# Rotary embedding joined in PSUM by TensorE, and GpSimd left with gathers only, in a two-layer diffusion backbone step

## The chip, the cores and the metric

One Trainium2 chip, one of its cores. The metric is the device time of one launch in microseconds (us): three runs of the kernel before took 4050.77, 4027.24 and 4058.07 us, median 4050.77. The profile comes from one more execution, which has its own time.

## The reference, cut to what matters

One inference step of two layers over 128 context tokens ("prompt") and 512 latent tokens ("sample"), width 1024, all in float32. Each layer is a mixer (layer 0: grouped-query attention and retention; layer 1: differential and windowed attention) followed by a PEER channel mixer, in which each token has 8 heads that choose 16 of 16384 single-neuron experts. What the change touches:

```python
def ada(x, gain, shift, scale):
    return rmsnorm(x, gain) * (1.0 + scale[:, None, :]) + shift[:, None, :]

def apply_rope(x, cos, sin):           # latent tokens only
    x1, x2 = x[..., :half], x[..., half:]
    return concatenate([x1 * cos - x2 * sin, x1 * sin + x2 * cos], axis=-1)

# retention, per chunk: qc * q_dec[..., None] meets the carried state s
o = intra + einsum('bhqd,bhdv->bhqv', qc * q_dec[..., None], s)

# PEER, per block of 128 tokens
a = einsum('td,thkd->thk', xb, u[ib])       # rows of u chosen by index
w = gb * gelu(a)
out = einsum('thk,thkd->td', w, v[ib])      # rows of v chosen by index
```

## The kernel before

Activations stand transposed, 128 features by tokens, in float32. The sample's projections split each operand into a rounded high part and a residue (`hhi`, `hlo`, `whi`, `wlo`) and take three TensorE matmuls for one product (L478). The program runs one after the other: mixer 0 (0 to about 716 us of the profile), routing 0 (to 1310), dense 0 (to 2200), mixer 1 (to 2640), routing 1 (to 3230) and dense 1 (to the end). The prompt's work is woven in between, and so are the gathers.

The PEER mixer is done in two ways. For three blocks of 128 sample tokens it multiplies densely with all experts (L1434, L1457). For the prompt's block and the last sample block, in each layer, it gathers the chosen rows: 128 rows of `u` per token and then 128 rows of `v`, each step an indirect DMA that GpSimd issues (L1323) into one of 8 buffers `row`, and one VectorE instruction of 128x1024 that consumes it (L1336 for `u`, L1340 for `v`). GpSimd may issue the next gather when VectorE has given a buffer back, so GpSimd, the DMA and VectorE form a ring. In mixer 1 VectorE consumes 171 gathers; in mixer 0 the ring runs from about 344 us on.

`chunk` (L558) loads a weight, projects into a PSUM bank of tag `mm` (two banks; the even mixer's q and k use tag `S`), runs the postponed work of the chunk before (`flush`, the list `pend`), and then hands the bank to its reader. The order on each engine is fixed when the program is built: a scheduler with a timeline of its own orders the instructions, and two pins keep gathers behind the instruction last written on GpSimd and VectorE (`after`, L1299).

Three jobs share GpSimd with the gathers:

- `rope` (L501), 18 times on the sample: 4 q chunks and k in mixer 0; k of the windowed attention and 4 times `cq`, `ck`, `dq` in mixer 1. `y` is in SBUF (VectorE scales it at L627 or L692 in mixer 0, ScalarE copies it out of PSUM at L957 in mixer 1). TensorE swaps the halves (`perm`, L505), GpSimd multiplies `y` by cos (L507), VectorE multiplies the swapped one by sin out of PSUM (L509), GpSimd adds (L511), in two instructions of 64 partitions where the two heads go to two tensors (`kz0`, `kz1`, and the two halves of `ck`).
- `qd` (L803): the decayed queries of the retention, 8 times in mixer 0.
- `hlo` of every third of the eight slices in `ada` (L446 to L450, `HL = 3`), 2 in each of the four sample norms, with a second ScalarE pass over the slice (L449). The other six are one VectorE instruction (L452).

Of the kernel before, what the change touches and what calls it, by code (L numbers as in the profile page):

```python
# [53 lines left out]
TRM = 1  # L54
RE = 1
DGB = 2
HL = 3
HN = 1
MHB = 1
ML = 1  # L60
# [96 lines left out]
def _consts():  # L157
    C = {}
    p = np.arange(128)
    C["ident"] = np.eye(128, dtype=np.float32)  # L160
    half = p // 64
    swap = p ^ 32
    perm = np.zeros((128, 128), np.float32)
    perm[swap, p] = 1.0
    C["perm"] = perm
    same = (half[:, None] == half[None, :]).astype(np.float32)
    C["center"] = (np.eye(128) - same / 64.0).astype(np.float32)
    sel = np.zeros((128, 2), np.float32)
    sel[p, half] = 1.0 / 64.0
    C["sel"] = sel  # L170
    inv = (np.float32(10000.0) ** (-np.arange(16, dtype=np.float32) / np.float32(16))).astype(np.float32)
    t = np.arange(NS)
    row = (t // 64).astype(np.float32)
    col = (t % 64).astype(np.float32)
    ang = np.concatenate([row[:, None] * inv, col[:, None] * inv], axis=-1).astype(np.float32)
    cos, sin = np.cos(ang).T, np.sin(ang).T
    d = p % 64
    C["cos"] = cos[d % 32].astype(np.float32)
    C["sin"] = (sin[d % 32] * np.where(d < 32, -1.0, 1.0)[:, None]).astype(np.float32)
    delta = np.arange(896)[None, :] - p[:, None] - 384  # L180
    C["delta"] = delta.astype(np.float32)
    C["qf"] = np.tile(np.arange(1, NS + 1, dtype=np.float32)[None], (128, 1))
    C["qb"] = np.tile((NS - np.arange(NS, dtype=np.float32))[None], (128, 1))
    C["kr"] = np.stack([127.0 - p, p], axis=1).astype(np.float32)
    kq = p[None, :] - p[:, None]
    C["mprev"] = np.where(kq >= 0, 0.0, NEG).astype(np.float32)
    C["mnext"] = np.where(kq <= 0, 0.0, NEG).astype(np.float32)

    first = [[o for o, ab in enumerate(CAND) if ab[0] == a][0] for a in range(16)]
    C["first"] = np.tile(np.array(first, np.float32)[None], (128, 1))  # L190
    C["firstk"] = np.tile(np.array(first, np.float16)[None, :, None], (128, 1, 16))
    C["iotak"] = np.tile(np.arange(16, dtype=np.float16)[None, :, None], (128, 1, 16))
    C["iota2"] = np.tile(np.arange(128, dtype=np.float16)[None, :, None], (128, 1, 2))
    return {k: np.ascontiguousarray(v) for k, v in C.items()}
# [54 lines left out]
class K:  # L249
# [186 lines left out]
    def ada(self, st, gs, sh):  # L436

        nc = self.nc
        r = st.r0 if st.r0 is not None else self.rstd_x(st)
        st.r0 = None  # L440
        pb = self.rstd_bcast(st, r)
        h = self.pair_tile(st, "h")
        for k in range(8):
            t = self.wk.tile([128, st.T], F32, tag="t2", name="ada_t", bufs=6)
            nc.vector.scalar_tensor_tensor(t, st.x[:, k], gs[:, k:k + 1], pb[:, :st.T], op0=ALU.mult, op1=ALU.mult)
            if st.sample:  # L446
                nc.scalar.activation(h[0][:, k], t, AF.Identity, bias=sh[:, k:k + 1])
                if HL and k % HL == HL - 1:
                    nc.scalar.activation(t, t, AF.Identity, bias=sh[:, k:k + 1])  # L449
                    nc.gpsimd.tensor_tensor(h[1][:, k], t, h[0][:, k], op=ALU.subtract)  # L450
                    continue
                nc.vector.scalar_tensor_tensor(h[1][:, k], t, sh[:, k:k + 1], h[0][:, k],  # L452
                                               op0=ALU.add, op1=ALU.subtract)
            else:
                nc.scalar.activation(h[:, k], t, AF.Identity, bias=sh[:, k:k + 1])
        return h
# [41 lines left out]
                nc.tensor.matmul(pb[w * g:w * g + w, i * 128:(i + 1) * 128], r[:, o + g:o + g + 1].to_broadcast([128, w]),  # L498
                                 self.c["ident"], start=True, stop=True, tile_position=(0, w * g))

    def rope(self, y, outs):  # L501

        nc, c = self.nc, self.c
        ps = self.bank("mm")
        nc.tensor.matmul(ps, c["perm"], y, start=True, stop=True)  # L505
        t1 = self.wk.tile([128, NS], F32, tag="t2", name="rp1", bufs=6)
        nc.gpsimd.tensor_tensor(t1, y, c["cos"], op=ALU.mult)  # L507
        t2 = self.wk.tile([128, NS], F32, tag="t2", name="rp2", bufs=6)
        nc.vector.tensor_tensor(t2, ps, c["sin"], op=ALU.mult)  # L509
        for dst, sl in outs:  # L510
            nc.gpsimd.tensor_tensor(dst, t1[sl], t2[sl], op=ALU.add)  # L511

    def vtrans(self, src, st, dsts):

# [91 lines left out]
    def even(self, sts):  # L606
# [10 lines left out]
        for m in (4, 0, 1, 2, 3):  # L617
            for st, p in self.chunk(sts, "win0", m, CS):
                n = 2 * st.nt
                if m == 4:  # L620
                    st.kraw = self.ph.tile([128, st.T], F32, tag="rq" + st.name, name="kraw", bufs=2)
                    st.sv = self.ph.tile([128, 5 * n], F32, tag="sv" + st.name, name="sv")
                if m == 4:
                    nc.vector.tensor_copy(st.kraw, p)
                else:
                    y = self.wk.tile([128, st.T], F32, tag="t2", name="y", bufs=6) if st.sample else st.mo[:, m]
                    nc.vector.tensor_scalar(y, p, c["gqk"][:, 0:1], None, op0=ALU.mult)  # L627
                sq = self.wk.tile([128, st.T], F32, tag="t2", name="sq", bufs=6)
                nc.scalar.activation(sq, p, AF.Square)

                def rest(st=st, sq=sq, m=m, n=n):
                    pv = self.small(st)
                    self.head_sums(pv, 0, sq, st, c["sel"])
                    nc.vector.tensor_copy(st.sv[:, m * n:(m + 1) * n], pv[:, :n])
                    if m == 3:
                        st.r = self.rsq(st.sv, 5 * n)
                        st.r8 = self.ph.tile([128, 5 * n], F32, tag="r8" + st.name, name="r8")
                        nc.vector.tensor_scalar(st.r8, st.r, 0.125, None, op0=ALU.mult)

                st.pend.append(rest)  # L640
                if m < 4 and st.sample:
                    st.pend.append(lambda y=y, st=st, m=m: self.rope(y, [(st.mo[:, m], slice(0, 128))]))
# [36 lines left out]
    def qk_finish(self, st, m):  # L679
# [10 lines left out]
        if st.sample:  # L690
            y = self.wk.tile([128, T], F32, tag="t2", name="y", bufs=6)
            nc.vector.scalar_tensor_tensor(y, raw, gain, pb[:, :T], op0=ALU.mult, op1=ALU.mult)  # L692
            self.rope(y, outs)
        else:
            for dst, sl in outs:
                nc.vector.scalar_tensor_tensor(dst, raw[sl], gain[sl], pb[sl, :T], op0=ALU.mult, op1=ALU.mult)
# [89 lines left out]
    def retention(self, st, cch):  # L786
# [4 lines left out]
        if st.sample:  # L791
# [5 lines left out]
            for d, rn in ((0, "qf"), (1, "qb")):  # L797
# [2 lines left out]
                dq = self.wk.tile([128, NS], F32, tag="t2", name="dq", bufs=6)  # L800
                nc.scalar.activation(dq, ramp, AF.Exp, scale=lg[:, 16 + 4 * d + cch:17 + 4 * d + cch])
                qd = self.wk.tile([128, NS], F32, tag="t2", name="qd", bufs=6)
                nc.gpsimd.tensor_tensor(qd, st.rq, dq, op=ALU.mult)  # L803
                nc.tensor.matmul(O, sbd[:, d], qd, start=d == 0, stop=False)
        for g in range(2):
            h = 2 * cch + g
# [146 lines left out]
    def rope_or_copy(self, st, p, outs, out):  # L953
        nc = self.nc
        if st.sample:
            y = self.wk.tile([128, st.T], F32, tag="t2", name="y", bufs=6)
            nc.scalar.copy(y, p)  # L957
            st.pend.append(lambda: self.rope(y, outs))
            return
        for dst, sl in outs:  # L960
# [792 lines left out]
```

## Time and profile before

| what | us |
|---|---|
| median of three runs | 4050.77 (4027.24 to 4058.07) |
| the profiled execution, its own time | 4050.72 |
| its span, first to last instruction | 4048.9 |
| TensorE busy | 3653.0 (90%) |
| VectorE busy | 3180.2 (79%) |
| ScalarE busy | 1620.7 (40%) |
| GpSimd busy | 1621.2 (40%) |
| mixer 0 / mixer 1 (stage lengths) | 716 / 440 |

Engines: PE is TensorE's matmuls, PEld its weight loads, DVE VectorE, ACT ScalarE, POOL GpSimd. A busy PE is not a PE at its peak, since matmuls are pipelined. A wait is idle time of an engine and what ended it. The chain is the work that ended last, followed back from the last instruction: a microsecond saved off the chain saves nothing.

### The profile page before, as it was taken

What the parts mean: (1) busy time and instruction counts of PE and PEld (TensorE: products, weight loads), DVE (VectorE), ACT (ScalarE), POOL (GpSimd) and SP (SyncE); (2) the same over time, 40 slices, a digit from 0 to 9 for tenths busy, and PEclk for the clock granted to TensorE, in tenths of its full rate; (3) what the DMA queues carried; (4) which work ended last, traced back from release to release, by engine and by line L of the source; (5) the groups of instructions that cost most, each with busy time, mean ns of one, the idle gap of its engine ahead of it and who ended that gap; (6) DMA issues with size and microseconds to landing.
All of it is one profiled execution on the core that took longest, in us unless ns stands there. A gap on an engine that the chain in (4) does not pass through costs nothing.

```text
span 4048.9 us, 57028 instructions
## 1 busy us (share of the span) xinstructions
PE 3653.0 (90%) x19986; PEld 3060.2 (76%) x19986; DVE 3180.2 (79%) x6370; ACT 1620.7 (40%) x2971; POOL 1621.2 (40%) x1138
## 2 busy tenths in 40 slices
PE   7888889889997999999998898988976999999998
PEld 3675556778886877888886676777875888888887
DVE  3238668999997767778897898899997667777777
ACT  3222223334776433433333333333476634333333
POOL 1004445320554234443464676532075233444342
PEclk9999989999998999999999999999997999999999
DMA  8556778775798889899896777777577889999886
GB/s 320 179 176 235 276 281 281 252 233 181 277 363 323 308 294 358 301 338 347 303 351 250 241 244 231 257 257 232 188 266 274 331 301 333 345 337 324 301 309 213
DMA packets 441087, 1134.86 MB, mean 280 GB/s; under 512 B 40640, under 2 KB 191360, under 8 KB 434528
## 3 DMA queue, kind: packets, MB, share of 16 engines
q0 software_dynamic: 147968, 537.36, 37.7%
q1 hardware_dynamic: 251408, 506.28, 36.3%
q10 hardware_dynamic: 41424, 87.57, 5.8%
q8 instruction: 157, 2.57, 0.2%
q14 instruction: 130, 1.06, 0.1%
HBM read 1045.08 MB, written 85.98 MB: 279 GB/s over the span
## 4 chain that ended last, share of the span: by engine, by line
PE 48%; DVE 16%; DMA 8%; issue 8%; ACT 5%; POOL 2%; ACTq 0%; DVEq 0%; POOLq 0%; SPq 0%
PE d L1457 21%; PE mm L1434 14%; PE mm L478 5%; DMA u<-ut 3%; DVE acc L1340 3%; DVE row L1336 2%; DMA row<-u,xi 2%; PE pm L482 2%; DVE ulo L1423 2%; ACT gst L1407 2%; POOL row L1323 1%; DMA Gd<-gst 1%; ACT uhi L1422 1%; PE S L708 1%; DMA Ad<-gpre 1%
## 5 line engine op out<-in xcount | busy, mean ns | idle before, releaser
L1323 POOL DMA_INDIRECT row<-v,xi x512 | 832.3, 1626 | 1114.1 <-DVE acc L1340 773.6
L1323 POOL DMA_INDIRECT row<-u,xi x512 | 681.3, 1331 | 789.0 <-DVE row L1336 585.2
L1434 PE MATMUL mm<-hhi,uhi 128*128 128x384 f32 x2048 | 709.6, 346 | 46.9 <-ACT uhi L1422 43.2
L1434 PE MATMUL mm<-hhi,ulo 128*128 128x384 f32 x2048 | 707.2, 346 | 49.3 <-DVE ulo L1423 49.1
L1434 PE MATMUL mm<-hlo,uhi 128*128 128x384 f32 x2048 | 702.6, 343 | 2.2 <-DVE hlo L452 1.6
L1336 DVE SCALAR_TENSOR_TENSOR row<-hn,row 128x1024 f32<-128x1024 f32 x512 | 630.0, 1257 | 47.4 <-DMA row<-u,xi 39.8
L1340 DVE SCALAR_TENSOR_TENSOR acc<-row,gw,acc 128x1024 f32<-128x1024 f32 x508 | 650.6, 1281 | 4.2 <-DMA row<-v,xi 1.6
L1457 PE MATMUL d<-vlo,Whi 128*128 128x512 f32 x1536 | 482.1, 394 | 5.6 <-DVE vlo L1498 5.6
L1457 PE MATMUL d<-vhi,Wlo 128*128 128x512 f32 x1536 | 479.0, 393 | 0.0
L1422 ACT CAST uhi<-u 128x1024 fp32r<-128x1024 f32 x256 | 268.8, 1050 | 491.8 <-PE mm L1434 226.8
L1423 DVE TENSOR_TENSOR ulo<-u,uhi 128x1024 fp32r<-128x1024 f32 x256 | 313.5, 1225 | 185.0 <-ACT uhi L1422 183.7
L1457 PE MATMUL d<-vhi,Whi 128*128 128x512 f32 x1536 | 437.3, 397 | 16.9 <-ACT vhi L1497 13.2
L1434 PEld LDWEIGHTS mm<-hhi,uhi 128*128 128x128 f32 x2048 | 396.5, 194 | 65.1 <-ACT uhi L1422 54.4
L1434 PEld LDWEIGHTS mm<-hhi,ulo 128*128 128x128 f32 x2048 | 395.3, 193 | 66.0 <-DVE ulo L1423 62.7
L1434 PEld LDWEIGHTS mm<-hlo,uhi 128*128 128x128 f32 x2048 | 395.2, 193 | 8.7 <-DVE hlo L452 2.0
L1457 PEld LDWEIGHTS d<-vhi,Whi 128*128 128x128 f32 x1536 | 288.1, 190 | 74.9 <-ACT vhi L1497 17.3
L1457 PEld LDWEIGHTS d<-vhi,Wlo 128*128 128x128 f32 x1536 | 288.0, 188 | 61.4 <-issue 0.2
L1457 PEld LDWEIGHTS d<-vlo,Whi 128*128 128x128 f32 x1536 | 286.4, 189 | 62.8 <-DVE vlo L1498 8.0
L1498 DVE TENSOR_TENSOR vlo<-v,vhi 128x1024 fp32r<-128x1024 f32 x256 | 312.2, 1221 | 14.2 <-ACT vhi L1497 13.9
L1505 ACT CAST Whi<-W 128x384 fp32r<-128x384 f32 x256 | 131.2, 513 | 433.1 <-PE d L1457 337.1
L1497 ACT CAST vhi<-v 128x1024 fp32r<-128x1024 f32 x256 | 268.5, 1051 | 53.3 <-DMA v<-v 41.9
L478 PE MATMUL mm<-hhi,whi 128*128 128x512 f32 x624 | 255.4, 410 | 31.5 <-DVE rvs L594 12.6
(470 smaller groups left out, 5776.4 us busy)
## 6 DMA issues: line engine op xcount, KB each, us to landing
u<-ut SPq DMA_DIRECT2D x256, 512.0 KB, 5.3
v<-v SPq DMA_DIRECT2D x256, 512.0 KB, 6.2
Gd<-gst ACTq DMA_DIRECT2D x48, 1024.0 KB, 8.7
G<-Gd SPq DMA_DIRECT2D x64, 768.0 KB, 8.8
w<-win SPq DMA_DIRECT2D x80, 512.0 KB, 4.7
w<-wq SPq DMA_DIRECT2D x64, 512.0 KB, 5.2
Ad<-gpre ACTq DMA_DIRECT2D x152, 192.0 KB, 4.5
pre<-Ad SPq DMA_DIRECT2D x152, 192.0 KB, 6.0
```

The source lines that it names most:

```text
L478: nc.tensor.matmul(ps[:, :st.T], wp[a][:, k], h[b][:, k], start=(n == 0), stop=(n == 23))
L482: nc.tensor.matmul(ps[:, :st.T], w32[:, k], h[:, k], start=(k == 0), stop=(k == 7))
L1323: nc.gpsimd.indirect_dma_start(out=r, out_offset=None, in_=self.A[f"{'uv'[n // 128]}{l}"], in_offset=bass.IndirectOffsetOnAxis(ap=xi[:, s: ...
L1336: nc.vector.scalar_tensor_tensor(r, hn, 1.0, r, op0=ALU.mult, op1=ALU.mult, accum_out=a[:, s:s + 1])
L1340: nc.vector.scalar_tensor_tensor(acc, r, w[:, s:s + 1], acc, op0=ALU.mult, op1=ALU.add)
L1422: nc.scalar.copy(hi, u)
L1423: nc.vector.tensor_tensor(lo, u, hi, op=ALU.subtract)
L1434: nc.tensor.matmul(ps[:, :ND], u[a][:, k], h[b][:, k, :ND], start=n == 0, stop=n == 23)
L1457: nc.tensor.matmul(acc[t][hf], a[:, ts], b[:, hf * 512:(hf + 1) * 512], start=(i == 0 and n == 0), stop=(i == 127 and n == 2))
L1497: nc.scalar.copy(vhi, v)
L1498: nc.vector.tensor_tensor(vlo, v, vhi, op=ALU.subtract)
L1505: nc.scalar.copy(whi, w)
```

## The change

`rope` is cut in two. `rope_parts` makes two VectorE products with cos and with sin, directly from the projection's PSUM bank (in mixer 0 with the gain in the same instruction); the y copy and GpSimd's product go. `rope` then has TensorE add them in one PSUM bank: the identity times the cos product, and the half-swap times the sin product, accumulated. ScalarE copies the sum to where it belongs. The sign of the sine table moves with the swap. `qd` is multiplied by VectorE, and `ada` makes all eight `hlo` on VectorE without the second ScalarE pass.

```diff
-HL = 3
-    C["sin"] = (sin[d % 32] * np.where(d < 32, -1.0, 1.0)[:, None]).astype(np.float32)
+    C["sin"] = (sin[d % 32] * np.where(d < 32, 1.0, -1.0)[:, None]).astype(np.float32)
...
                 nc.scalar.activation(h[0][:, k], t, AF.Identity, bias=sh[:, k:k + 1])
-                if HL and k % HL == HL - 1:
-                    nc.scalar.activation(t, t, AF.Identity, bias=sh[:, k:k + 1])
-                    nc.gpsimd.tensor_tensor(h[1][:, k], t, h[0][:, k], op=ALU.subtract)
-                    continue
                 nc.vector.scalar_tensor_tensor(h[1][:, k], t, sh[:, k:k + 1], h[0][:, k],
                                                op0=ALU.add, op1=ALU.subtract)
...
-    def rope(self, y, outs):
+    def rope_parts(self, y, gain=None):
+        nc, c = self.nc, self.c
+        parts = []
+        for nm in ("cos", "sin"):
+            t = self.wk.tile([128, NS], F32, tag="t2", name="rp" + nm, bufs=6)
+            if gain is None:
+                nc.vector.tensor_tensor(t, y, c[nm], op=ALU.mult)
+            else:
+                nc.vector.scalar_tensor_tensor(t, y, gain, c[nm], op0=ALU.mult, op1=ALU.mult)
+            parts.append(t)
+        return parts
+
+    def rope(self, parts, outs):
         nc, c = self.nc, self.c
         ps = self.bank("mm")
-        nc.tensor.matmul(ps, c["perm"], y, start=True, stop=True)
-        t1 = self.wk.tile([128, NS], F32, tag="t2", name="rp1", bufs=6)
-        nc.gpsimd.tensor_tensor(t1, y, c["cos"], op=ALU.mult)
-        t2 = self.wk.tile([128, NS], F32, tag="t2", name="rp2", bufs=6)
-        nc.vector.tensor_tensor(t2, ps, c["sin"], op=ALU.mult)
+        nc.tensor.matmul(ps, c["ident"], parts[0], start=True, stop=False)
+        nc.tensor.matmul(ps, c["perm"], parts[1], start=False, stop=True)
         for dst, sl in outs:
-            nc.gpsimd.tensor_tensor(dst, t1[sl], t2[sl], op=ALU.add)
+            nc.scalar.copy(dst, ps[sl])
...
             y = self.wk.tile([128, T], F32, tag="t2", name="y", bufs=6)
             nc.vector.scalar_tensor_tensor(y, raw, gain, pb[:, :T], op0=ALU.mult, op1=ALU.mult)
-            self.rope(y, outs)
+            self.rope(self.rope_parts(y), outs)
...
-                nc.gpsimd.tensor_tensor(qd, st.rq, dq, op=ALU.mult)
+                nc.vector.tensor_tensor(qd, st.rq, dq, op=ALU.mult)
...
-            y = self.wk.tile([128, st.T], F32, tag="t2", name="y", bufs=6)
-            nc.scalar.copy(y, p)
+            y = self.rope_parts(p)
             st.pend.append(lambda: self.rope(y, outs))
```

GpSimd's queue at the start of mixer 1, before, around the ropes of the first `cq` and `ck`. A row is one instruction, with what it waits for; DMASW0 to DMASW7 are the eight queues of the gathers.

```order
L507 TENSOR_TENSOR rp_19987<-y,c_cos 128x512 [waits DMAHW5_49,DMAHW2_49,DMAHW7_49,DMAHW0_49,Activation_49]
L1323 DMA row<-u,xi 128x1024 [waits DVE_49] x2
L507 TENSOR_TENSOR rp_20036<-y,c_cos 128x512 [waits Activation_49]
L511 TENSOR_TENSOR cqs<-rp_19987,rp_19989 128x512 [waits DMAHW0_49,DVE_49,Pool_49]
L1323 DMA row<-u,xi 128x1024
L1323 DMA row<-u,xi 128x1024 [waits DVE_49]
L1323 DMA row<-u,xi 128x1024 [waits DMASW0_49,DVE_49]
L511 TENSOR_TENSOR cks<-rp_20036,rp_20038 64x512 [waits DVE_49,Pool_49]
L511 TENSOR_TENSOR cks<-rp_20036,rp_20038 64x512 [waits DMASW4_49,DMASW3_49,DMASW5_49,DMASW2_49,DMASW6_49,DMASW1_49,DMASW7_49,DMASW0_49,Pool_49]
L1323 DMA row<-u,xi 128x1024 [waits Pool_49]
```

The same queue now, over the whole of mixer 1's first three head groups (xN is N instructions in a row):

```order
L931 MEMSET cks 64x640 x4
L1331 DMA row<-u,xi 128x1024 x30
L931 MEMSET cks 64x640 x2
L1331 DMA row<-u,xi 128x1024 x34
L931 MEMSET cks 64x640 x2
```

No elementwise instruction is left between the gathers, and the instruction that waited for all eight gather queues is gone (it stood five times in mixer 1: once for `kz1`, four times for `ck`).

VectorE's queue at the same place, before (`wlo` is the residue of the next weight; `vs` and `cvs` are values):

```order
L1336 SCALAR_TENSOR_TENSOR row,ga<-hn,row 128x1024 x3
L468 TENSOR_TENSOR wlo<-w_20003,whi 128x1024
L509 TENSOR_TENSOR rp_19989<-mm,c_sin 128x512
L1336 SCALAR_TENSOR_TENSOR row,ga<-hn,row 128x1024 x3
L468 TENSOR_TENSOR wlo<-w_20053,whi 128x1024
L509 TENSOR_TENSOR rp_20038<-mm,c_sin 128x512
L1336 SCALAR_TENSOR_TENSOR row,ga<-hn,row 128x1024 x3
L468 TENSOR_TENSOR wlo<-w_20604,whi 128x1024
```

And now:

```order
L504 TENSOR_TENSOR rpcos<-mm,c_cos 128x512
L504 TENSOR_TENSOR rpsin<-mm,c_sin 128x512
L1344 SCALAR_TENSOR_TENSOR row,ga<-hn,row 128x1024 x3
L464 TENSOR_TENSOR wlo<-w_19994,whi 128x1024
L1344 SCALAR_TENSOR_TENSOR row,ga<-hn,row 128x1024 x2
L504 TENSOR_TENSOR rpcos<-mm,c_cos 128x512
L504 TENSOR_TENSOR rpsin<-mm,c_sin 128x512
L1344 SCALAR_TENSOR_TENSOR row,ga<-hn,row 128x1024 x4
```

Each rope has two products, which read the projection's own bank and stand right behind it; runs of up to four gathered rows stand ahead of the next pair.

## Rows read from the trace of the kernel before

**Rows 1.** The page: its first lines (span; busy time and share of each engine).

```profile
span 4048.9 us, 57028 instructions
...
PE 3653.0 (90%) x19986; PEld 3060.2 (76%) x19986; DVE 3180.2 (79%) x6370; ACT 1620.7 (40%) x2971; POOL 1621.2 (40%) x1138
```

**Rows 2.** Busy time by engine in stages; columns named in its first line.

```profile
core 0: us, PE busy (x) PEld busy (x) DVE busy (x) ACT busy (x) POOL busy (x), PEclk, DMA share, GB/s
0.00:716.00 716.00, 618.43 (x3683) 408.57 (x3683) 410.49 (x991) 208.06 (x439) 234.07 (x211) 0.93 0.72 250
716.00:1310.00 594.00, 515.49 (x3207) 475.51 (x3208) 546.89 (x1368) 320.67 (x634) 218.60 (x129) 0.93 0.77 269
...
2200.00:2640.00 440.00, 383.08 (x1890) 290.02 (x1888) 373.45 (x679) 155.15 (x350) 279.53 (x207) 0.95 0.71 240
2640.00:3230.00 590.00, 491.32 (x3033) 450.56 (x3034) 534.04 (x1382) 305.03 (x606) 222.58 (x125) 0.91 0.75 259
```

**Rows 3.** GpSimd by form, 2200 to 2640: xcount, busy us, mean ns, idle before.

```profile
L507 POOL TENSOR_TENSOR rp<-y,c_cos 128x512 f32<-128x512 f32 x13 | 18.0, 1386 | 6.5 <-ACT y L957 4.4 <-issue 1.7
L511 POOL TENSOR_TENSOR cks<-rp,rp 64x512 f32<-64x512 f32 x8 | 13.4, 1673 | 12.9 <-DMA row<-u,xi 9.7 <-DVE dg L741 3.1
```

**Rows 4.** The same, GpSimd, 0 to 716.

```profile
L803 POOL TENSOR_TENSOR qd<-rqs,dq 128x512 f32<-128x512 f32 x8 | 11.0, 1376 | 19.3 <-ACT rqs L662 13.4 <-ACT dq L801 5.8
```

**Rows 5.** VectorE by form, 2200 to 2640.

```profile
L1336 DVE SCALAR_TENSOR_TENSOR row<-hn,row 128x1024 f32<-128x1024 f32 x128 | 166.1, 1329 | 10.9 <-DMA row<-u,xi 10.9
...
L468 DVE TENSOR_TENSOR wlo<-w,whi 128x1024 fp32r<-128x1024 f32 x26 | 41.3, 1592 | 0.6 <-ACT whi L467 0.6
...
L509 DVE TENSOR_TENSOR rp<-mm,c_sin 128x512 f32<-128x512 f32 x13 | 8.9, 686 | 6.5 <-PE mm L505 4.2 <-POOL rp L507 2.3
...
L452 DVE SCALAR_TENSOR_TENSOR hlo<-ada_t,mod,hhi 128x512 fp32r<-128x512 f32 x6 | 6.3, 1083 | 0.1
```

**Rows 6.** VectorE by form, 0 to 716.

```profile
L1336 DVE SCALAR_TENSOR_TENSOR row<-hn,row 128x1024 f32<-128x1024 f32 x128 | 157.8, 1254 | 15.5 <-DMA row<-u,xi 15.4
L468 DVE TENSOR_TENSOR wlo<-w,whi 128x1024 fp32r<-128x1024 f32 x30 | 36.8, 1231 | 50.3 <-ACT whi L467 47.7 <-DMA out_new_rb<-ssb 2.2
...
L885 DVE TENSOR_TENSOR hlo<-xs,hhi 128x512 fp32r<-128x512 f32 x8 | 5.3, 688 | 0.0
```

**Rows 7.** Single lines, whole run: ns min/median/max, then first and last start.

```profile
L1336 DVE SCALAR_TENSOR_TENSOR row<-hn,row x512: 1153/1220/2795, 349.7 to 3571.1; 128x1024 f32<-128x1024 f32 x171
...
L468 DVE TENSOR_TENSOR wlo<-w,whi x88: 1194/1220/2318, 26.5 to 2786.4; 128x1024 fp32r<-128x1024 f32 x88
...
L505 PE MATMUL mm<-y,c_perm x36: 590/592/1222, 181.4 to 2524.9; 128*128 128x512 f32 x36
...
L957 ACT COPY y<-mm x13: 564/579/582, 2230.5 to 2515.3; 128x512 f32<-128x512 f32 x13
```

**Rows 8.** Timeline from 2399.4: start us, us, instruction.

```profile
2399.46 1.38 POOL L507 TENSOR_TENSOR rp<-y,c_cos 128x512 f32<-128x512 f32 x1 [1.67 <-ACT y L957]
...
2399.63 2.30 DVE L468 TENSOR_TENSOR wlo<-w,whi 128x1024 fp32r<-128x1024 f32 x1
```

**Rows 9.** Chain that ended last, 2200 to 2640, by line.

```profile
by line: DVE row L1336 17.3%; DMA row<-u,xi 14.4%; PE mm L478 11.4%; issue 8.8%; PE S L708 6.8%; PE tr L756 3.6%; POOL row L1323 3.5%; PE acc L1007 3.2%; DVE wlo L468 2.5%; PE mm L756 2.1%; PE tr L1042 1.9%; DVE mx L1085 1.7%; PE S L1075 1.
```

**Rows 10.** The same chain, pieces: start us, us, what.

```profile
2266.71 1.53 POOL cks L511
...
2268.28 2.12 PE S L708 x4
```

**Rows 11.** Waits in mixer 1, PE then VectorE: us, times, longest us.

```profile
PE S L708 <- POOL cks L511: 4.1, 1, 4.1
...
PE S L708 <- POOL cks L511: 2.8, 1, 2.8
...
DVE row L1336 <- DMA row<-u,xi: 10.9, 9, 4.8
```

More of the change, by code (lines that the diff above doesn't have):

```diff
@@ L625, in even @@
                 else:
-                    y = self.wk.tile([128, st.T], F32, tag="t2", name="y", bufs=6) if st.sample else st.mo[:, m]
-                    nc.vector.tensor_scalar(y, p, c["gqk"][:, 0:1], None, op0=ALU.mult)
+                    if st.sample:
+                        y = self.rope_parts(p, c["gqk"][:, 0:1])
+                    else:
+                        nc.vector.tensor_scalar(st.mo[:, m], p, c["gqk"][:, 0:1], None, op0=ALU.mult)
                 sq = self.wk.tile([128, st.T], F32, tag="t2", name="sq", bufs=6)
```

## Prediction, made before the run

> **What bounds the kernel now.** I read the page first, then the table of stages, then chain, waits and groups inside the two mixers, the only stages with ropes. Over the span of 4048.9 us TensorE is busy for 90% and VectorE for 79% [rows 1], but the shares differ by stage [rows 2]. In mixer 0 (716 us) TensorE is busy for 618.4 us, VectorE for 410.5: a TensorE stage. In routing 0 VectorE is busy for 546.9 of 594 us. In mixer 1 (440 us) neither is full: TensorE 383.1, VectorE 373.5, GpSimd 279.5. There the chain says what ends last [rows 9]: VectorE's gathered rows 17.3%, the landing of gathers 14.4% and GpSimd's issue of them 3.5%, so 35.2% lies in the gather ring; TensorE's groups of 1.9% or more (11.4, 6.8, 3.6, 3.2, 2.1, 1.9) make 29.0%. So I price mixer 1 by both.
>
> For a microsecond of work added to or taken from an engine I count the share of its busy time that lies on the chain. TensorE in mixer 1: 29.0% of 440 us is 128 us of 383, so 0.33. VectorE: 17.3, 2.5 and 1.7% make 21.5%, 95 us of 373, so 0.25 [rows 2, 9]. That is a choice; the ends are 0 and 1.
>
> **The change in mixer 1, part by part.**
>
> TensorE. A rope's matmul is two passes of 592 ns, 36 for 18 ropes [rows 7]; a second one per rope adds 1.18 us, 13 times here: +15.4 us of work, times 0.33 = **+5.1** (0 to +15.4).
>
> VectorE, more work. The sine product from PSUM takes 686 ns [rows 5], and 13 cosine products of the same shape from PSUM come on top: +8.9. Two `hlo` at 1083 ns: +2.2. Together +11.1 us.
>
> VectorE, less stretching. A `wlo` that starts at 2399.63, while GpSimd multiplies from 2399.46 to 2400.84, takes 2.30 us [rows 8]; its median is 1.22 [rows 7]. The groups show how often: the gathered rows average 1329 ns in mixer 1 against their median of 1220, 128 times: 14.0 us; `wlo` 1592 against 1220, 26 times: 9.7 us [rows 5, 7]. In mixer 0, with ropes ahead of the gathers and only 8 `qd` beside them, the means are 1254 and 1231 [rows 6]. I take all of it, −23.6 us (the other end is `wlo` alone, −9.7, which would leave +1.4 net). Net −12.5, times 0.25 = **−3.1**.
>
> The Trainium skill, page "SBUF — State Buffer", section "Who interferes with whom", says that a VectorE instruction with two SBUF inputs and a GpSimd one that reads SBUF share one read port, and that the loser blocks for the whole instruction. By that rule alone each of the 13 rope products and 8 half adds on `ck` could cost VectorE its full length, 31.4 us [rows 3], not the 23.6 us read from the means; the sum below would be 2 us lower. The row above agrees with the rule in size (1.08 us more than the median), not in every collision; I keep the row.
>
> GpSimd's late `ck`. The second half of a rope's add waited for all gather queues to land; TensorE's scores then waited for it. Of four such waits two are on the chain: the score at 2268.28 starts 0.04 us after the add that began at 2266.71 ended [rows 10], having waited 4.1 us, and the one near 2433 waited 2.8 [rows 11]. ScalarE now copies out of PSUM right behind TensorE, with a projection still to run, and waits for no gather. **−6.9** (0 to −11). What is late next is the softmax loop, which is dependent work.
>
> Gathers. GpSimd loses its elementwise work (ropes' products and half adds alone 31.4 us [rows 3]) and the full drains of the queue. VectorE sat idle for 10.9 us waiting for rows of `u` here [rows 11]; the chain holds 14.4% of 440, 63 us, of such landings, most of which are latency that another path would replace. I take **−10.9**; ends 0 and −63.
>
> ScalarE. 13 copies of `y` (579 ns [rows 7]) become 18 copies out of PSUM, +2.9 us on an engine busy for 155 of 440 us [rows 2]: nothing. If that cover is gone, 2.9.
>
> Mixer 1: 5.1 − 3.1 − 6.9 − 10.9 = −15.8.
>
> **Mixer 0.** Five ropes add 5 × 1.18 = 5.9 us to TensorE, busy for 618 of 716, so times 0.86: **+5.1** (0 to 5.9). VectorE: the q ropes swap one product of 128x512 for another; k's gets one more, +0.7; 8 `qd` by the 688 ns of a 128x512 with two SBUF inputs [rows 6], +5.5; two `hlo`, +2.2; stretching gone, 128 × 34 ns and 30 × 11 ns [rows 6, 7], −4.7. Net +3.7 on an engine that is idle for 43% of the stage; at 0.25, **+0.9**. GpSimd loses 11.0 us of `qd` [rows 4], which I count at nothing, since the gathers there run far ahead of the end of the stage.
>
> **Routings.** In each, the opening norm has two `hlo` more on VectorE, 2.2 us; at 0.25 **+1.1** for both. ScalarE saves its second pass, hidden behind VectorE. The dense stages contain nothing of the change, and the count of gathers consumed by the start of either dense stage is as before. The order of independent instructions there shifts in places; I price that at 0, within some us either way.
>
> **Sum.** 4050.7 (the profiled execution's own time, which is also the median of the three runs) − 15.8 + 5.1 + 0.9 + 1.1 = 4042.0 us, 0.2% less. One per cent, 40 us, is about what a measurement of this kernel can tell from no change: its own three runs lie 31 us apart.
>
> **The rivals.**
>
> *A. TensorE waits for VectorE's products (slower).* Before, ScalarE freed the projection's bank in 0.58 us [rows 7]. Now two VectorE products of 0.69 must end first, in a queue that is 85% busy [rows 2] and has runs of three or four gathered rows ahead of them, 3.7 to 4.9 us each at 1.22 [rows 7]. There are two `mm` banks, and the rope's sum takes one of them. If the wait comes out at the whole run for each of the 13 ropes, 13 × 3.7 = 48 us are lost on TensorE: 4090. It decides from the point at which the products end later than the work that TensorE has between them, one projection of 24 matmuls. Against it: the scheduler put the products where it expects the bank, and attention work lies between. Chance 0.12.
>
> *B. The gather ring leaves the chain altogether (faster).* Half of the 63 us of landings goes, not 10.9: 20.6 us more, 4021; with every stretched instruction of VectorE on the chain (weight 1 instead of 0.25, 9.4 us more) 4012. For it: 35.2% of mixer 1's chain is in the ring, and each drain of the queue empties it. Against it: VectorE itself waited only 10.9 us for landings, and TensorE, with 383 + 15 of 440 us, has little more to give. Chance 0.18.
>
> *C. Gain and cost cancel.* TensorE's 21.3 us of added matmuls (15.4 + 5.9) all count, while the ring yields nothing: 4050.7 + 21.3 − 6.9 − 3.1 + 2.0 = 4064. For it: TensorE is the fullest engine of the whole [rows 1]. Against it: in mixer 1 it is idle for 57 us, waiting. Chance 0.20.
>
> The forecast has 0.50, with a range of its own of 4030 to 4055.
>
> **How the numbers follow.** The forecast is the likeliest case, 4042. The range takes in C and most of B, and cuts A's upper half: 4010 to 4072. Faster by over 1% is under 4010, B's far end with the spread of runs: 0.10. Slower by over 1% is over 4091, A's far end: 0.07. Within 1%: 0.83.
>
> **What the profile after would show.** Right: mixer 1 some 15 us shorter; the gathered rows and `wlo` there at means near 1.23 us; no score waiting for a `ck` from GpSimd; landings a smaller share of mixer 1's chain; mixer 0 some 6 us longer with TensorE fuller. Wrong: TensorE idle ahead of the identity matmul or a projection, released by a cosine or sine product (A); mixer 1 shorter by 30 us or more (B); mixer 1 no shorter although the stretching is gone (C); a change of over 10 us in a dense stage, which none of my terms reaches.

## The result, and the profile after

The changed kernel takes 4023.63 us (median of 18 runs), the kernel before 4049.07 (18 runs beside them): ratio 0.9941, 95% interval 0.9929 to 0.9953. One of the 18 took 8403.42 us, twice as long as any other, at a granted clock that was no lower; the ratio leaves it out as slow, and its cause is open. The change is thus 0.6% faster, where 0.2% was forecast: 18 us below the forecast of 4042, inside its range of 4010 to 4072, and by the text's own bound within 1%. The sign and the class hold. The terms of the sum mostly do not, as the profile shows.

The page of the kernel after, first lines (to be read against [rows 1]):

```profile
span 4022.4 us, 57005 instructions
...
PE 3638.6 (90%) x20022; PEld 3053.5 (76%) x20022; DVE 3159.0 (79%) x6400; ACT 1621.1 (40%) x2974; POOL 1486.9 (37%) x1080
```

GpSimd is busy for 134 us less and VectorE for 21 us less, yet the span fell by 26.5. To see where, I cut both spans at the same events: the first matmul that broadcasts a norm opens mixer 0, routing 0, mixer 1 and routing 1, and the first matmul into the output banks opens each dense stage. Busy time by engine in these six stages, the kernel before (the columns are those of [rows 2]: the stage's length, then busy us of PE, PEld, DVE, ACT and POOL, PE's granted clock, DMA share, GB/s):

```profile
25.10:717.90 692.80, 609.30 (x3629) 404.54 (x3629) 409.52 (x979) 198.15 (x416) 224.39 (x187) 0.93 0.71 247
717.90:1310.90 593.00, 515.51 (x3206) 475.60 (x3206) 546.20 (x1366) 320.22 (x632) 217.01 (x128) 0.93 0.77 269
1310.90:2209.20 898.30, 860.15 (x4429) 749.23 (x4427) 705.98 (x1184) 342.78 (x544) 373.26 (x257) 0.99 0.90 321
2209.20:2642.20 433.00, 379.17 (x1870) 288.52 (x1870) 366.60 (x668) 149.95 (x342) 274.29 (x209) 0.95 0.71 239
2642.20:3267.10 624.90, 521.64 (x3205) 479.34 (x3205) 542.93 (x1389) 318.68 (x631) 221.93 (x124) 0.91 0.73 254
3267.10:4048.90 781.80, 757.25 (x3592) 658.10 (x3592) 606.42 (x770) 279.66 (x383) 299.02 (x211) 0.98 0.90 313
```

and the kernel after:

```profile
23.70:705.50 681.80, 599.19 (x3639) 399.49 (x3639) 406.35 (x990) 200.12 (x420) 198.71 (x163) 0.94 0.72 251
705.50:1293.40 587.90, 512.73 (x3204) 474.96 (x3205) 544.28 (x1366) 318.62 (x630) 198.00 (x126) 0.93 0.77 271
1293.40:2196.60 903.20, 861.44 (x4429) 749.53 (x4427) 707.62 (x1183) 343.54 (x545) 362.46 (x258) 0.99 0.90 320
2196.60:2626.20 429.60, 380.62 (x1896) 290.37 (x1896) 350.48 (x687) 152.40 (x345) 223.04 (x175) 0.96 0.72 242
2626.20:3236.50 610.30, 516.86 (x3206) 478.05 (x3206) 542.29 (x1392) 317.77 (x629) 195.77 (x122) 0.92 0.74 260
3236.50:4022.40 785.90, 757.74 (x3592) 656.68 (x3592) 605.41 (x770) 277.35 (x383) 297.05 (x211) 0.98 0.89 311
```

The differences, beside the prediction's terms:

| stage | predicted | profiles |
|---|---|---|
| mixer 0 | +6.0 | −11.0 |
| routing 0 | +0.5 | −5.1 |
| dense 0 | 0 | +4.9 |
| mixer 1 | −15.8 | −3.4 |
| routing 1 | +0.5 | −14.6 |
| dense 1 | 0 | +4.1 |

How far such a row can be trusted: two kernels were profiled twice (the changed one, and the one with the norm and `qd` edits alone). Their mixers repeated within 2.3 us, their routings within 1.2, their dense stages within 6.4. So the dense rows say nothing, and three rows want a cause: mixer 0 shorter instead of longer, mixer 1 hardly shorter, routing 1 shorter by 15 us although next to nothing changed in it. I do not follow up routing 0: all other kernels below, the null among them (590.2), have it at 584.5 to 590.9 us, so most of its 5.1 us lies with the one profile of the kernel before.

What the prediction said of VectorE in mixer 1 did come. VectorE by form there, after (against [rows 5]):

```profile
L1344 DVE SCALAR_TENSOR_TENSOR row<-hn,row 128x1024 f32<-128x1024 f32 x125 | 148.3, 1219 | 21.4 <-DMA row<-u,xi 21.4
...
L464 DVE TENSOR_TENSOR wlo<-w,whi 128x1024 fp32r<-128x1024 f32 x24 | 29.1, 1219 | 0.2
...
L504 DVE TENSOR_TENSOR rpcos<-mm,c_cos 128x512 f32<-128x512 f32 x13 | 8.9, 683 | 11.4 <-PE mm L474 11.4
```

The gathered rows fell from a mean of 1329 ns to 1219 and `wlo` from 1592 to 1219: with GpSimd's elementwise work gone, these means are down at the medians of [rows 7]. VectorE's busy time fell by 16.1 us in the stage, where −12.5 was worked out. The stage became only 3.4 us shorter. And the first row shows what did not come: VectorE waits 21.4 us for landings of gathers, against 10.9 before [rows 11].

### The profile page after: what moved, and what is told of

It reads as the page before. It is cut to its first block, busy times and chain, and to the rows that moved or that the text cites. A ratio compares the mean times of both kernels' runs of the same rounds, so it can differ in the third digit from the quotient of the medians.

```text
span 4022.4 us, 57005 instructions
## 1 busy us (share of the span) xinstructions
PE 3638.6 (90%) x20022; PEld 3053.5 (76%) x20022; DVE 3159.0 (79%) x6400; ACT 1621.1 (40%) x2974; POOL 1486.9 (37%) x1080
## 5 line engine op out<-in xcount | busy, mean ns | idle before, releaser
L1331 POOL DMA_INDIRECT row<-v,xi x512 | 778.1, 1520 | 1205.5 <-DVE acc L1348 866.7
L1344 DVE SCALAR_TENSOR_TENSOR row<-hn,row 128x1024 f32<-128x1024 f32 x512 | 610.3, 1218 | 50.8 <-DMA row<-u,xi 40.4
L1506 DVE TENSOR_TENSOR vlo<-v,vhi 128x1024 fp32r<-128x1024 f32 x256 | 311.9, 1219 | 23.5 <-ACT vhi L1505 23.2
```

The lines of the kernel that those rows point to most:

```text
L1331: nc.gpsimd.indirect_dma_start(out=r, out_offset=None, in_=self.A[f"{'uv'[n // 128]}{l}"], in_offset=bass.IndirectOffsetOnAxis(ap=xi[:, s: ...
L1344: nc.vector.scalar_tensor_tensor(r, hn, 1.0, r, op0=ALU.mult, op1=ALU.mult, accum_out=a[:, s:s + 1])
L1506: nc.vector.tensor_tensor(vlo, v, vhi, op=ALU.subtract)
```

## The experiments

Twelve kernels, in the order of the questions. Each ratio compares with runs of the kernel before on the same chip, and can differ by about 0.001 from the quotient of the two medians. "Stage" always means the six stages above, and a stage's length is that of one profiled execution.

### The three edits one by one

**Only `qd` on VectorE:**

```diff
-                nc.gpsimd.tensor_tensor(qd, st.rq, dq, op=ALU.mult)
+                nc.vector.tensor_tensor(qd, st.rq, dq, op=ALU.mult)
```

> The kernel before, with one edit: the 8 decayed queries (qd) are multiplied by VectorE. Theory P (the prediction's terms): it costs VectorE 5.5 us in mixer 0 and gives nothing, so the time stays within 3 us of before. Theory Q (read from the two traces: in mixer 0 the matmuls on qd follow one another after 92.6, 85.4 and 82.8 us before, and after 80.4, 86.0 and 78.4 us with the change): gathers stand in GpSimd's queue behind a qd that waits for ScalarE, so qd alone shortens mixer 0 by 10 to 16 us and the total by as much. Stages other than mixer 0 should stay within 3 us.

4042.41 us, ratio 0.9975 (0.9961 to 0.9989). Mixer 0 takes 678.7 us, 14 less than before, and the total falls by about 10.

**Only the ropes** (the change without its edits to `HL` and `qd`):

```diff
-    def rope(self, y, outs):
+    def rope_parts(self, y, gain=None):
...
+    def rope(self, parts, outs):
```

> The kernel before, with the rope edit alone; qd and every third norm residue stay on GpSimd. Theory P: mixer 1 is 15.8 us shorter, mixer 0 about 5 us longer, total 9 to 11 us less than before. Theory Q: mixer 0 before the gathers start is 3 to 4 us longer, mixer 1 is 3 to 4 us shorter, total within 3 us of before.

4042.32 us, ratio 0.9973 (0.9958 to 0.9988). Mixer 0 takes 688.0 us, mixer 1 431.1. The total is what theory P said, but not for its reason: mixer 1 is 1.9 us shorter than before, not 15.8. The profiled execution took 4050.24 us, 8 more than the median, so its stages do not show where the 0.27% went.

**Only the norm residues:**

```diff
-HL = 3
+HL = 0
```

> The kernel before, with one edit: all norm residues on VectorE, no second ScalarE pass. Theory P: 1 us per norm more on VectorE, total +1 to +2 us. Theory Q: the four openings of stages lose the wait for a GpSimd instruction that stands behind gathers, 1 to 3 us each in the two routings and in mixer 1, total 4 to 8 us less; the routings hold it (routing 0 and 1 were 5 and 15 us shorter with the whole change).

4027.93 us, ratio 0.9939 (0.9919 to 0.9959): the edit that was priced at +1.1 us yields as much alone as the whole change does, several times what theory Q allowed. Routing 1 takes 609.5 us.

**A null:** two VectorE memsets of 128x512 that nobody reads, ahead of mixer 0's decays.

```diff
+        for _ in range(2):
+            nc.vector.memset(self.wk.tile([128, 512], F32, tag="t2", name="pad", bufs=6), 0.0)
```

> The kernel before with two idle VectorE memsets of 128x512 (under 1 us) ahead of the decay constants; no work is moved. It shifts the scheduler's times and so the order on all engines. If order alone can shorten the routings or the mixers (theory R), a stage moves here by 5 us or more without cause; by theories P and Q the total stays within 3 us of before and every stage within 4 us, which is then the bound for reading stages in one profile each.

4054.41 us, ratio 1.0006 (0.9992 to 1.002). Its stages: mixer 0 687.7 us, mixer 1 435.3, routing 1 623.8. Mixer 0 is 5 us off the kernel before, the shift that theory R named, so order alone moves a stage by that much, and I compare the others with both.

### Routing 1: order or work?

The norm edit takes two GpSimd subtractions and two ScalarE passes out of routing 1's opening, and it also makes the scheduler weave the stage otherwise. On ScalarE's queue the dense stage's prepared blocks (`uhi`) are laid between the copies of the gate tables (`gst`): before, 11 of 77 blocks are left when the last gate copy has been issued; with the norm edit 4 are. To tell the two apart, one kernel gets the order without the work being moved, and one the work without the order.

**The kernel before with one idle memset** after routing 1's norm, GpSimd's subtractions kept:

```diff
+        if st.sample:
+            self.nada = getattr(self, "nada", -1) + 1
...
+        if st.sample and self.nada == 3:
+            nc.vector.memset(self.wk.tile([128, 512], F32, tag="t2", name="pad", bufs=6), 0.0)
```

> The kernel before, with nothing moved: one idle VectorE memset of 128x512 (under 0.5 us) behind the norm that opens routing 1. It makes the scheduler weave that stage as in the changed kernel: 4 instead of 11 of the 77 dense blocks made ahead are left when the last gate block is built. Theory R (order): routing 1 takes 608 to 613 us instead of 625, and the total is 10 to 18 us under before, as far as the change itself goes there. Theory S (the norm's work leaving GpSimd shortens routing 1): the work is still there, so routing 1 stays at 624 to 627 us and the total within 3 us of before.

4031.10 us, ratio 0.9956 (0.9942 to 0.9970), with 4 blocks left; routing 1 takes 609.4 us.

**The whole change, but routing 1's norm as before:**

```diff
...
+                if self.nada == 3 and k % 3 == 2:
+                    nc.scalar.activation(t, t, AF.Identity, bias=sh[:, k:k + 1])
+                    nc.gpsimd.tensor_tensor(h[1][:, k], t, h[0][:, k], op=ALU.subtract)
+                    continue
```

> The whole change, but in the norm that opens routing 1 every third residue stays on GpSimd with its second ScalarE pass. The order of that stage is then that of before (11 blocks left at the end). Theory R: routing 1 is back at 624 to 627 us and the total is 10 to 15 us above the changed kernel, 4034 to 4040. Theory S with the work as cause says the same of this kernel; with e5 the two part. By the prediction's terms the total is 4023, 1 us under the changed kernel.

4031.33 us, ratio 0.9965 (0.9952 to 0.9979), with 11 blocks left; routing 1 takes 619.2 us.

So the order brings the 15 us: an instruction that does nothing is enough. Without that order 9 of them are lost again, fewer than the 624 to 627 us of the expectation would have it; where the other 5 or 6 come from is open. (A long gather issue on GpSimd mostly comes and goes with this order; the last section weighs it.) Every kernel with 11 blocks left has a routing 1 of 619 to 627 us, every one with 4 or 5 left one of 608 to 611. Where in the stage: busy time by engine, from 400 to 500 us after its opening, in the null:

```profile
3039.40:3139.40 100.00, 61.21 (x455) 56.45 (x455) 76.81 (x127) 60.96 (x155) 43.78 (x31) 0.76 0.78 282
```

and in the kernel with the one memset:

```profile
3045.00:3145.00 100.00, 71.64 (x526) 67.51 (x527) 76.95 (x126) 60.07 (x146) 43.71 (x27) 0.81 0.79 279
```

VectorE and ScalarE are as busy in both. TensorE does 10 us more work there: beside as many of the gate's matmuls (257 and 256), which wait for the other two engines, stand 227 matmuls of the independent blocks instead of 155.

### Mixer 0: what `qd` held up

**`qd` on VectorE, GpSimd as busy as before:** in its place GpSimd makes a product of two constants of the same shape, which waits for nothing and which nobody reads, pinned at that point of its queue (6 of the 8 stand between gathers).

```diff
-                nc.gpsimd.tensor_tensor(qd, st.rq, dq, op=ALU.mult)
+                nc.vector.tensor_tensor(qd, st.rq, dq, op=ALU.mult)
+                idle = self.ph.tile([128, NS], F32, tag="idle", name="idle", bufs=1)
+                with self.after(POOL):
+                    nc.gpsimd.tensor_tensor(idle, c["cos"], c["sin"], op=ALU.mult)
```

> The kernel before with qd on VectorE, as e1, but GpSimd makes an idle product of the same size (cos times sin) each time, 6 of the 8 between gathers, that waits for nothing. Theory Q1 (the gathers stood behind a qd that waits for ScalarE): the gain of e1 stays, total 4038 to 4046, mixer 0 at 676 to 683 us. Theory Q2 (GpSimd's time and VectorE's stretching were the cost): the gain goes, total 4047 to 4054, mixer 0 at 685 to 693 us.

4034.70 us, ratio 0.9974 (0.9960 to 0.9988); mixer 0 takes 679.1 us, as with `qd` moved alone (678.7). So the gain is not GpSimd's time, nor the stretching of VectorE by its products. All five kernels with `qd` on GpSimd have a mixer 0 of 685 to 693 us, all nine profiles with it on VectorE one of 675 to 682. What it held up is harder to say. One wait of TensorE's changes in most kernels: for the retention's values `rvs`, which VectorE copies out of a projection's bank. Waits of PE from 320 to 700 us, before:

```profile
PE mm L478 <- DVE rvs L594: 12.6, 3, 6.0
```

and with `qd` on VectorE alone:

```profile
PE mm L478 <- DVE rvs L594: 4.5, 2, 3.1
```

With GpSimd still making `qd` it is 12.4 us in the null, 12.0 with the one memset and 11.7 with the ropes alone; with `qd` moved 4.8 in the kernel of this section and 4.5 to 6.9 in the others but one. In front of that copy VectorE has gathered rows in its queue, and the gathers stand on GpSimd behind a `qd` that waited for ScalarE [rows 4]. That would make a path, but the runs do not show that it is the one. The kernel with the norm edit alone keeps `qd` on GpSimd, waits only 2.6 us there, and has a mixer 0 of 685.2 us; the one with a single matmul per rope, further down, has `qd` moved, waits 10.5, and has one of 677.5. And TensorE's idle time over the whole of mixer 0 does not account for the gain. The null, then the kernel of this section:

```profile
23.20:710.90 687.70, 603.34 (x3629) 399.98 (x3628) 410.49 (x981) 198.18 (x416) 225.52 (x187) 0.94 0.73 250
24.00:703.10 679.10, 598.93 (x3629) 397.97 (x3629) 413.58 (x987) 198.44 (x416) 224.05 (x185) 0.95 0.73 253
```

TensorE is idle for 84.4 us in the first and 80.2 in the second, so half of the 8.6 us lies in its busy time. With `qd` moved alone it is 76.9, but between the stage tables before and after, where the stage is 11 us shorter, it falls only from 83.5 to 82.6. The granted clock does not sort the kernels either; it is 0.95 with the ropes alone, whose mixer 0 is 688.0 us. That a `qd` on GpSimd costs mixer 0 about 9 us is shown; its path is open.

### What the ropes are worth

**The norm and `qd` edits without the ropes:**

```diff
-HL = 3
+HL = 0
...
-                nc.gpsimd.tensor_tensor(qd, st.rq, dq, op=ALU.mult)
+                nc.vector.tensor_tensor(qd, st.rq, dq, op=ALU.mult)
```

(against the kernel before)

> The kernel before with two of the three edits: qd on VectorE and all norm residues on VectorE; ropes as before. If the parts add up (e1 gave 0.25%, e3 0.61%), 4015 to 4022, which is less than the changed kernel, and the rope edit then costs a few us on top of them. If the rope edit carries its own 0.27% as it did alone, this kernel comes out at 4028 to 4036, above the changed kernel. By the prediction's terms it would be 4052.

4001.71 us, ratio 0.9883 (0.9862 to 0.9905), below all that was expected: leaving out the largest edit makes it better. That was another chip than the changed kernel's, so the last four ran together, on one chip.

**The changed kernel again** (no edit):

> The changed kernel itself, beside the next three on one chip, so that they can be compared without going through different chips. Two theories of the rope edit. Theory T: its added TensorE matmuls (21.3 us in all by the prediction) lie on the path and it gives nothing back, so the whole change costs 10 to 25 us against the kernel without the rope edit. Theory N: the rope edit neither costs nor gains, and the difference seen so far (0.9941 against 0.9883, on different chips) is spread between chips and runs. Both expect 0.993 to 0.996 of the kernel before here, about 4022 us.

4019.03 us, 0.9928 (0.9903 to 0.9952).

**The norm and `qd` edits again** (the edit above):

> The norm and qd edits without the rope edit, again, beside the changed kernel on one chip. Theory T: 10 to 25 us less than the changed kernel, ratio to before 0.987 to 0.991. Theory N: within 6 us of the changed kernel, ratio 0.992 to 0.996.

4006.05 us, 0.9881 (0.9855 to 0.9908).

**The same with the rope edit in mixer 1 alone:**

```diff
...
-            y = self.wk.tile([128, st.T], F32, tag="t2", name="y", bufs=6)
-            nc.scalar.copy(y, p)
-            st.pend.append(lambda: self.rope(y, outs))
+            y = self.rope_parts(p)
+            st.pend.append(lambda: self.rope_join(y, outs))
```

> The norm and qd edits, and the rope edit in mixer 1 alone (13 of 18 ropes); the five ropes of mixer 0 stay on GpSimd (a subtraction there, since the sine table has the other sign). By the prediction's terms (5.1 less 3.1, 6.9 and 10.9 us) this edit in mixer 1 gains 15.8 us against the norm and qd edits alone. Theory T: it costs 13/18 of the difference between the changed kernel and the norm and qd edits, 7 to 18 us, and mixer 1 is 0 to 10 us longer. Theory N: within 6 us of both.

3997.12 us (3989.11 to 4000.65), 0.987 (0.9848 to 0.9892): the lowest median of all kernels here, and its slowest run is faster than any run of the changed kernel (4007.55 to 4026.33). From the kernel just above it is not clear of noise: two of that one's six runs (3986.07 and 3995.76) are below its median.

**The changed kernel with one matmul per rope:**

```diff
-        nc.tensor.matmul(ps, c["ident"], parts[0], start=True, stop=False)
-        nc.tensor.matmul(ps, c["perm"], parts[1], start=False, stop=True)
+        nc.tensor.matmul(ps, c["perm"], parts[1], start=True, stop=True)
```

> The changed kernel with one of the rope's two matmuls taken out (the identity times the cosine product; both VectorE products are still made, so the rope leaves out its cosine half), so TensorE has as much work in a rope as the kernel before. Theory T: it gains back 10 to 21 us on the changed kernel. Theory N, or a cost of the rope edit that is not the matmul (the two products on VectorE, the copies out of PSUM, the order): within 6 us of the changed kernel.

4017.19 us, 0.9919 (0.9897 to 0.9941), 2 us from the changed kernel.

Both theories fall. Theory T (the matmuls cost) fails twice: without the second matmuls 2 us are gained, not 10 to 21, and no cost of mixer 1's ropes is seen; with them the stage is 6.2 us shorter (429.7 to 423.5) and the median 9 us lower, if within the noise. Theory N fails with the 22 us between the third kernel and the first, which differ in the five ropes of mixer 0.

The profile shows a part of those 22 us, and not in mixer 0, but at the opening of mixer 1. VectorE there, in the changed kernel (start us, us, instruction, idle before it):

```profile
2189.48 1.15 DVE L1344 SCALAR_TENSOR_TENSOR row<-hn,row 128x1024 f32<-128x1024 f32 x1
...
2192.86 2.35 DVE L464 TENSOR_TENSOR wlo<-w,whi 128x1024 fp32r<-128x1024 f32 x2
2196.28 0.18 DVE L419 RECIPROCAL r<-r 128x4 f32<-128x4 f32 x1 [1.06 <-ACT r L417]
2203.65 1.22 DVE L1344 SCALAR_TENSOR_TENSOR row<-hn,row 128x1024 f32<-128x1024 f32 x1 [7.20 <-DMA row<-u,xi]
...
2204.80 4.03 DVE L445 SCALAR_TENSOR_TENSOR ada_t<-xs,gs,mm 128x512 f32<-128x512 f32 x6
```

and GpSimd:

```profile
2190.92 5.11 POOL L1331 DMA_INDIRECT row<-u,xi  x1 [7.38 <-DVE row L1344]
2196.34 0.94 POOL L1331 DMA_INDIRECT row<-u,xi  x1 [0.30 <-issue]
2197.58 0.94 POOL L1331 DMA_INDIRECT row<-u,xi  x1 [0.30 <-issue]
```

One gathered row stands on VectorE between the norm's reciprocal and the norm's first slice, `ada_t`. Its gather is still under way, VectorE stands for 7.2 us, and with it the norm and TensorE. TensorE's waits for the norm, at the stage's opening:

```profile
PE mm L474 <- ACT hhi L447: 8.6, 1, 8.6
PE mm L474 <- DVE hlo L448: 3.5, 1, 3.5
```

In the kernel with the rope edit in mixer 1 alone the gathers were issued ahead of that run of VectorE, and the wait for a row is 1.63 us:

```profile
2173.45 0.94 POOL L1339 DMA_INDIRECT row<-u,xi  x1 [0.30 <-DVE xs L1277]
```

```profile
2181.80 1.22 DVE L1352 SCALAR_TENSOR_TENSOR row<-hn,row 128x1024 f32<-128x1024 f32 x1 [1.63 <-DMA row<-u,xi]
...
2185.35 4.04 DVE L445 SCALAR_TENSOR_TENSOR ada_t<-xs,gs,mm 128x512 f32<-128x512 f32 x6 [2.23 <-PE mm L410]
```

```profile
PE mm L478 <- DVE hlo L452: 2.4, 1, 2.4
...
PE mm L478 <- ACT hhi L447: 1.6, 1, 1.6
```

So TensorE loses 12.1 us here in the changed kernel and 4.0 in this one. It goes by kernel, not by run: 11.3 to 12.5 us in the five profiles with mixer 0's ropes on the new path, 7.7 to 8.1 in the kernel before, the null, the one memset and the two with only `qd` moved, 4.0 in the four others, which have the norm edit and mixer 0's ropes as before. (With the norm edit alone the row stands ahead of the reciprocal instead, and TensorE waits 8.9 us just before the stage's first matmul; before the change 3.8 us fall there, in the changed kernel 1.4.) What differs between the kernels is the place of a few gathered rows in VectorE's queue.

With this opening taken off, mixer 1 is easier to read. Its length less these two waits is 417.1 to 419.8 us in all six kernels and profiles with the new ropes there (mean 418.1) and 424.2 to 429.0 in the eight without (mean 426.4). By these means the rope edit is worth 8 us in mixer 1, and the opening gives 4.4 of it back against the kernel before (7.7 to 12.1).

What is left of the 22 us, some 14, lies in mixer 0 (679.5 against 674.7 us) and dense 0 (901.2 against 895.9) of two single profiles. For dense 0 that is within what one kernel differs from itself, and the kernel without any rope edit has a mixer 0 of 678.7 and 679.9. I leave its cause open.

## Why the prediction was right, and where it was not

That the total was right in sign and class is luck: large errors of both signs met. By the profiles, mixer 0 and the routings gained 38 us more than forecast, mixer 1 gained 12 less, and the dense stages with the first microseconds came out 8 longer, which leaves 18.

**Mixer 1, TensorE +5.1: wrong, it is not seen.** With one matmul per rope the stage, less its opening, takes 417.4 us, and with two 417.2. The size was off as well. A pass is recorded with 592 ns, but the two passes of a rope's second matmul start 0.86 us after those of the first:

```profile
2239.37 1.02 PE L515 MATMUL mm<-rpcos,c_ident 128*128 128x512 f32 x2
2240.23 1.02 PE L516 MATMUL mm<-rpsin,c_perm 128*128 128x512 f32 x2
```

so a second one costs 0.86 us here, not 1.18. And the weight of 0.33, TensorE's share of the chain, was no price for this microsecond: as I read it, the matmuls went where TensorE waits anyway.

**VectorE −3.1: its busy time right, its worth unknown.** −16.1 us measured for −12.5 worked out; of the 23.6 us of stretching all went. The rule of the Trainium skill on the shared port (page "SBUF — State Buffer", section "Who interferes with whom") agrees: means of 1329 and 1592 ns became 1219 when GpSimd's elementwise work beside them was gone. The 31.4 us that the prediction worked out by the rule left out GpSimd's other adds in the same stretch, 15.9 us. How much of the 16.1 us VectorE was waited for, no run here tells.

**The late `ck` −6.9: the wait is gone as said.** No wait of TensorE for a `ck` is left in the stage. Together with the term before (−3.1 − 6.9 = −10.0) it comes near the 8 us that the ropes bring; no run takes the two apart.

**Gathers −10.9: wrong.** This is the step that failed for mixer 1. The prediction took VectorE's 10.9 us of waiting for rows as time that a freed GpSimd would give back. VectorE's waits for landings grew instead, to 21.4 us, of which 7.2 stand at the opening. With the same good opening they are 7.0 us without the new ropes and 12.8 with them. GpSimd itself waits in this stage for VectorE to give buffers back, 95.6 us behind rows in the changed kernel (35 times) against 36.3 before (16 times): the ring went at VectorE's pace, not at GpSimd's. Landings did lose their place on the chain, as the prediction's list of signs has it. The changed kernel's own chain does not reach back to mixer 1, but that of the whole change with routing 1's norm as before does:

```profile
by line: PE mm L480 24.2%; DVE row L1350 15.8%; DMA row<-u,xi 9.1%; issue 6.3%; PE S L723 4.1%; DVE mx L732 3.3%; ACT P L741 3.1%; PE tr L1056 3.0%; PE tr L771 2.4%; PE acc L1021 2.2%; DVE wlo L470 2.1%; PE S L1089 2.0%; PE acc L1076 1.9%; 
```

In that execution landings make 9.1% instead of 14.4% [rows 9], and the projections' matmuls 24.2% instead of 11.4: another path took the place of the latency, as the prediction said of most of it, and the stage won little. With one matmul per rope the landings make 12.5%.

**Mixer 0, `qd` at nothing: wrong.** The prediction kept [rows 4], with 19.3 us of GpSimd's waiting ahead of `qd`, and counted it at nothing "since the gathers there run far ahead of the end of the stage". With `qd` on VectorE the stage is about 9 us shorter than in the null, also when GpSimd stays as busy. So the step that failed is to count a wait on GpSimd at nothing because the gathers have time; what it held up is not shown (the wait for `rvs` is a candidate, with two kernels against it). **TensorE's +5.1 there** is not seen: 687.7 us in the null and 688.0 with the ropes alone.

**Routings +1.1, order at 0: wrong, and the largest single error.** The order that the norm edit brings was worth 15 us in routing 1. The work of the two `hlo`, priced at 0.5 us there, was not measured by itself.

**The rivals.** A did not happen: TensorE's waits for the products are 0.4 us in mixer 1, and in mixer 0 one of 3.8. B's total (4021) came nearly true, but not by its mechanism: mixer 1 is 3.4 us shorter, not 30, and rows with their landings still make 24.9% of the chain above, against 31.7 before. C was half right, in that the ring yielded next to nothing, and wrong in that no cost of TensorE's matmuls is seen.

## What to carry to other kernels

Do not price a small instruction on a queue of fixed order by its duration alone, nor at nothing because its engine has time: `qd`, 11 us of work on an engine that is 40% busy, cost its stage about 9 us, and an idle product of the same length in its place cost nothing. Where a scheduler lays out the order, run a null that adds an idle instruction before crediting an edit with a gain, and split an edit by the stages it touches: here an idle memset was worth 0.4%, and the change without its ropes in mixer 0 (0.987) beat the whole (0.993 on the same chip).

## What the runs showed of the hardware

A gather's issue on GpSimd can last as long as a run of several VectorE instructions. The 5.11 us of the issue above (its median is 1.26) lie under VectorE's run of three rows and two `wlo`, which begins at 2189.48 and ends at 2195.21; the issue ends 0.82 us later. The next issue, at 2196.34, is that of the gather that VectorE then waits for, so VectorE held up its own row. The longest case is in routing 1 of the kernel before, 25.93 us:

```profile
2986.50 25.93 POOL L1323 DMA_INDIRECT row<-v,xi  x1 [4.09 <-DVE acc L1340]
```

```profile
3009.71 1.31 DVE L1340 SCALAR_TENSOR_TENSOR acc<-row,gw,acc 128x1024 f32<-128x1024 f32 x1
3010.90 0.71 DVE L1393 TENSOR_TENSOR gej<-c_iota,gbj 128x1024 f16<-128x1024 f16 x1
3011.51 1.99 DVE L1198 TENSOR_REDUCE pra<-ppr 128x64 f32<-128x1024 f32 x1
```

From 2986 on VectorE runs almost only instructions with two inputs in SBUF, one right after the other; at 3011.51 comes a reduction with one input, and the issue ends 0.92 us after that starts, which is what an undisturbed issue takes (0.94). The end is as sharp elsewhere. Of the 455 issues of rows that take over 3 us in the 14 profiles of this case, 446 end 0.81 to 0.83 us after the end of some VectorE instruction, and the other nine 0.72 to 0.74. After which one is not clear: in 368 of them VectorE goes on at once with an `acc`, which has two inputs in SBUF as well.

The same section of the Trainium skill says that a DMA that seems stalled by VectorE is one issued by GpSimd, which was starved of port time for its descriptors; the trace agrees. It also says that `tensor_tensor` was not seen to stall a DMA; here the trace differs, since the last 2.35 us of VectorE's run over the 5.11 us issue are two `wlo`, which are `tensor_tensor`. The length, up to 28 times an undisturbed issue, I had not expected. It was not tested by a run of its own.

Whether such an issue has a part in routing 1's 15 us is not settled, because the order that changes the blocks changes it too. Four kernels with 11 blocks left have one of 25.9 us in that stage, and the ropes alone one of 21.3; with 4 or 5 blocks left the longest there is 6.3 to 12.2 us. But the whole change with routing 1's norm as before has 11 blocks left, no issue over 8.4 us there, and a routing 1 of 619.2, against 620.6 in the kernel with the idle product, which has the long one. So 9 of the 15 us are there without it.
